# The first 512 columns of the gate's v input: seven block products in four steps among q and k, and their layer norm on VectorE

## The chip, the cores and the metric

The kernel runs on one core of a Trainium2 chip. The metric is the device time of one execution in microseconds. Before the change it is 2023.53 us, the median of three runs (2023.32 to 2023.73). TensorE (PE in the profile) multiplies; VectorE (DVE), ScalarE (ACT) and GpSimd (POOL) prepare its operands and take its results from the accumulators in PSUM; SyncE (SP) issues the loads of the weights.

## The reference, cut to what matters

A trunk of two layers on 256 positions of width 2048, all in float32. What the change touches is the first projection of each layer and the gate fed by its last columns:

```
for l in range(DEPTH):                      # 2
    h = rms_norm(x, norm1_g[l])             # (1, 256, 2048)
    z = h @ w_in[l]                         # w_in[l]: 2048 x 5120
    q, k, v, gu, gv = jnp.split(z, splits, axis=-1)     # 1024 columns each
    attn = dilated_attention(rotary(q), rotary(k), v)   # 8 heads of 128
    gm = chunked_gmlp(gelu(gu), gelu(gv), ln_g[l], ln_b[l], w_spatial[l], b_spatial[l])
    x = x + concat([attn, gm]) @ w_out[l]
    x = x + square(relu(rms_norm(x, norm2_g[l]) @ w_up[l])) @ w_down[l]

def chunked_gmlp(u, v, ln_g, ln_b, w_s, b_s):
    v = layer_norm(v in 8 groups of 128 columns, ln_g, ln_b)
    sp = (lower triangle of w_s) @ v + b_s  # in each group and each chunk of 128 positions
    return u * sp
```

The first 512 columns of gv are the first four of its eight groups.

## The kernel before, in words

**Three products for one.** Every weight tile is 128 x 1024 float32 (512 KB). SP loads it into `raw` (7 buffers); ACT rounds it to a high part `hi` (`Sub.high`, 6 buffers), VectorE subtracts and rounds to a low part `lo` (`Sub.low`, 6 buffers). PE forms hi·hi, lo·hi and hi·lo in its rounded float32. The activations have such parts as well: `hs` holds x times the norm's gain in both.

**A list of steps.** The function `layer` writes a list `steps`; the loop at the end walks it, and every engine gets its instructions in that order and executes them in that order. Each step issues, in turn: the high parts of tiles up to five ahead, whatever `soon` has made due, the low parts up to four ahead, the loads, its own matmuls, and then what hangs on it (`after`, hooks, and the queue that `later` fills). A mark is a step with no tile. An instruction that has to wait holds up all that stands behind it on its engine.

**Kinds of steps.** `transposed` has the weights stationary: one tile is 24 matmuls of 256 columns, four tiles make a group of 256 output columns. `natural` has the activations stationary: one tile is 12 matmuls of 512 columns into two accumulators, eight tiles make 512 output columns. `fast` forms a product of 2 x 2 blocks with seven block products for eight: a step loads two tiles (`Top`, `Bottom`), makes two more from their sums (`Sums`, upper and lower: four subtractions of 512 elements on VectorE, then high and low parts), and runs 42 matmuls of 256 columns; the last two are issued inside the next step. It needs activations and their block sums in high and low parts. Before the change only the second MLP product uses it, with block sums of the hidden activations that `sums` makes.

**The first stage of a layer.** v runs first (`natural`, 16 tiles), then k and q by turns (`transposed`, 4 groups each, 32 tiles; I call them places 0 to 31), then gv (`natural`, 16 tiles), then gu (`transposed`, 16 tiles), then the product with `w_out`. When a q or k group ends, `after_qk` rotates it (two ACT copies, three VectorE operations); two steps behind a q group `scores` runs, then `normalise`, `turn` and `values` for that pair of heads. When half of gv ends, `after_gv` takes it out of PSUM and through the gelu; `stats` and `layer_norm` follow, `layer_norm` on POOL; `spatial` (PE) needs the normed groups while gu runs.

**Accumulators.** PSUM has eight banks of 512: `acc0` to `acc3` for the steps, four `aux` for the small products of the attention and the norms.

Of the kernel before, what the change touches and what calls it, by code (L numbers as in the profile page):

```python
# [68 lines left out]
BEHIND, BETWEEN = 2, 1  # L69
D_SCORES, D_NORM, D_TURN, D_VALUES = 2, 1, 3, 2  # L70
# [21 lines left out]
def trunk(ctx: ExitStack, tc: tile.TileContext, layout, xT, consts, gains, w, b_sp, w_sp, out):  # L92
# [9 lines left out]
    paux = ctx.enter_context(tc.tile_pool(name="paux", bufs=4, space=bass.MemoryType.PSUM))  # L102
# [37 lines left out]

    def aux_bank():
        return paux.tile([P, 512], F32, name="aux", tag="aux")
# [223 lines left out]
    def sums_ready():  # L366
        run_until(lambda: summed[0])
# [46 lines left out]
    def fast(name, l, row0, col0, tiles, slots, fresh, last, done):  # L414
# [6 lines left out]
        for p in range(2):  # L421
# [3 lines left out]
            def mm(p=p, top=top, bottom=bottom, upper=upper, lower=lower):  # L425
                if p == 0:
                    o.extend(slots())
                half = tiles[0][0]
                sums_ready()
                extra = sum_parts[0]  # L430
# [44 lines left out]
    def mark(fn):  # L475

        steps.append((None, fn, None))

# [39 lines left out]
    def layer(l, n1, n2, n3, last):  # L518
# [27 lines left out]
        if l:  # L546
            mark(start)
        mix_a, mix_g = [None], [None]
# [38 lines left out]
        def scores(j, q, k):  # L587
# [3 lines left out]
            s1, s0 = aux_bank(), aux_bank()  # L591
# [65 lines left out]
        def after_gv(c, ps):  # L657
            z, u = t32("gz", [2, 512], tag="tmpB"), t32("gu", [2, 512], tag="tmpA")
            for tt in range(2):
                act.activation(z[:, tt, :], ps[tt], AF.Copy, scale=n1.half[:, tt:tt + 1])  # L660

            def then(u, z):
# [5 lines left out]
                later(1, 1.5, lambda: stats(c // P))  # L668

            gelu(z, u, then)  # L670

        def stats(g0):
# [8 lines left out]
            later(0, 1.0, lambda: layer_norm(g0))  # L681

        def layer_norm(g0):
            y, mv = par["y"], par["mv"]
            r = t32("lr", [2, 4])
            rsqrt(nc.gpsimd, r, mv[:, :, g0:g0 + 4, 1], 1.0, LN_EPS, [2, 4])
            for g in range(4):
                for tt in range(2):
                    yg = y[:, tt, (g0 + g) * P:(g0 + g + 1) * P]
                    nc.gpsimd.tensor_scalar(yg, yg, mv[:, tt, g0 + g, 0:1], r[:, tt, g:g + 1],  # L690
                                            op0=OP.subtract, op1=OP.mult)
# [108 lines left out]
        def sums():  # L800

            a11, a12, a21, a22 = (inner[:, 4 * k:4 * k + 4, t * P:(t + 1) * P] for t in range(2) for k in range(2))
            vec.tensor_tensor(a22, a21, a22, op=OP.add)
            vec.tensor_tensor(a21, a11, a21, op=OP.subtract)
            vec.tensor_tensor(a11, a22, a11, op=OP.subtract)
            vec.tensor_tensor(a12, a12, a11, op=OP.subtract)
# [41 lines left out]

        def halves(bank):
            return [bank[:, 0:256], bank[:, 256:512]]  # L850
# [62 lines left out]
        for e in range(9):  # L913
# [5 lines left out]
            if e:  # L919
                w = 512 * len(ORDER.get(e, USUAL))  # L920
                hidden = [hid[e - 1]]
                down = collect(transposed, "w_down", l, (e - 1) * 1024, 8, w, D - w, from_tiles(hidden, NH),
# [3 lines left out]
                for g, at in enumerate(ORDER.get(e, USUAL)):  # L926
                    banks = []
                    quick += zip(at, collect(fast, "w_down", l, (e - 1) * 1024, 512 * g, hidden,
# [16 lines left out]
    def hook(i, fn):  # L945

        hooks.setdefault(i, []).append(fn)
# [128 lines left out]
```

## Time and profile before

| | |
|---|---|
| median of three runs | 2023.53 us |
| profiled execution: its own time / its span | 2023.7 us / 2021.9 us |
| granted TensorE clock, mean of the span | 0.997 |
| busy PE / DVE / ACT / POOL | 99% / 78% / 60% / 8% of the span |
| weights loaded | 731 tiles of 512 KB, 4.7 us from issue to landing (median) |
| HBM read and written over the span | 206 GB/s |

The page is of one execution. "Busy" is the time in which an engine executes; on PE, matmuls overlap, so that a busy PE can still be slowed by what feeds it, but not stand. An answer by windows gives, for a stretch of the span, the busy time and the instruction count of each engine; a timeline gives start, length, engine, line and shape of every instruction, and in brackets the idle time ahead of it with what ended it.

### The profile page before, as it was taken

Reading aid. Unit: us, or ns where it says so; the run is one execution under the profiler, and the core shown is the slowest. Engines: PE = TensorE matmul, PEld = TensorE weight load, DVE = VectorE, ACT = ScalarE, POOL = GpSimd, SP = SyncE. Lnnn points to the kernel's source line nnn. Section 1 sums busy time; section 2 is a strip of 40 time slices with the busy share of each in tenths; the row PEclk is TensorE's granted clock in tenths of the full one; section 3 lists DMA queues with packets and bytes.
Section 4 is the critical chain, followed back from the end, with each engine's and each line's share of the span. In section 5 each row is a group of like instructions: output and inputs, shape, how many; then the busy total and the mean of one; then the engine's idle time right before and its main releaser. Section 6 shows DMA issues by size and latency. Waiting matters only on the chain.

```text
span 2021.9 us, 40716 instructions
## 1 busy us (share of the span) xinstructions
PE 2009.5 (99%) x16810; PEld 1973.4 (98%) x16810; DVE 1579.8 (78%) x1954; ACT 1221.2 (60%) x1613; POOL 156.2 (8%) x200
## 2 busy tenths in 40 slices
PE   9999999999999999999999999999999999999997
PEld 8998999999999999999989989999999999999997
DVE  7566766688888898898856667667888898888985
ACT  7565455566566666665645654556666666667653
POOL 0002300000001000100000032000000000010000
PEclk9999999999999999999999999999999999999998
DMA  9555556566678776866664555565676776777662
GB/s 330 192 167 167 187 189 202 174 229 204 222 219 239 240 225 203 249 215 215 201 215 158 168 187 188 188 199 179 217 229 208 228 236 216 239 220 241 212 215 81
DMA packets 126442, 419.26 MB, mean 207 GB/s; under 512 B 14128, under 2 KB 22064, under 8 KB 126256
## 3 DMA queue, kind: packets, MB, share of 16 engines
q1 hardware_dynamic: 110800, 389.86, 57.2%
q0 software_dynamic: 14304, 23.86, 6.5%
q8 instruction: 131, 2.15, 0.4%
q10 hardware_dynamic: 1152, 2.94, 0.4%
q14 instruction: 55, 0.45, 0.1%
HBM read 394.58 MB, written 22.02 MB: 206 GB/s over the span
## 4 chain that ended last, share of the span: by engine, by line
PE 99%; DVE 0%; ACT 0%; issue 0%; DVEq 0%
PE acc L410 70%; PE acc L440 10%; PE aux L440 8%; PE acc L470 3%; PE acc L472 3%; PE acc L471 3%; PE aux L699 0%; PE aux L635 0%; PE aux L593 0%; PE aux L622 0%; PE aux L994 0%; DVE x L1038 0%; PE aux L596 0%; PE aux L637 0%; PE acc L846 0%; PE aux L539 0%
## 5 line engine op out<-in xcount | busy, mean ns | idle before, releaser
L168 ACT ACTIVATE hi<-raw 128x1024 fp32r<-128x1024 f32 (+1 forms) x817 | 836.9, 1050 | 487.5 <-DVE raw L220 216.2
L178 DVE TENSOR_TENSOR lo<-raw,hi 128x1024 fp32r<-128x1024 f32 (+1 forms) x817 | 965.3, 1214 | 143.4 <-ACT hi L168 140.4
L410 PE MATMUL acc<-hs,hi 128*128 128x256 f32 x5632 | 985.9, 277 | 0.0
L410 PEld LDWEIGHTS acc<-hs,hi 128*128 128x128 f32 x5632 | 857.9, 188 | 0.4 <-issue 0.2
L410 PE MATMUL acc<-hs,lo 128*128 128x256 f32 x2816 | 778.0, 276 | 0.0
L410 PEld LDWEIGHTS acc<-hs,lo 128*128 128x128 f32 x2816 | 528.7, 188 | 0.4 <-issue 0.2
L410 PE MATMUL acc<-half,hi 128*128 128x256 f32 x2688 | 462.2, 276 | 0.0
L410 PEld LDWEIGHTS acc<-half,hi 128*128 128x128 f32 x2688 | 406.7, 188 | 0.0
L410 PE MATMUL acc<-half,lo 128*128 128x256 f32 x1344 | 371.0, 276 | 0.0
L410 PEld LDWEIGHTS acc<-half,lo 128*128 128x128 f32 x1344 | 252.3, 188 | 0.0
L873 POOL DMA_DIRECT2D far<-ar x92 | 74.2, 816 | 1164.4 <-ACT ar L876 563.9
L440 PE MATMUL acc<-hi,shared 128*128 128x256 f32 x768 | 138.4, 276 | 0.0
L440 PEld LDWEIGHTS acc<-hi,shared 128*128 128x128 f32 x768 | 119.2, 188 | 0.0
L440 PE MATMUL aux<-hi,half 128*128 128x256 f32 x528 | 110.6, 276 | 0.0
L440 PE MATMUL acc<-lo,shared 128*128 128x256 f32 x384 | 106.0, 276 | 0.0
L649 DVE TENSOR_TENSOR half<-ar,half 128x512 fp32r<-128x512 f32 x72 | 49.8, 691 | 68.6 <-ACT half L646 68.6
L470 PE MATMUL acc<-hi,hs 128*128 128x512 f32 x256 | 101.8, 398 | 0.0
L472 PE MATMUL acc<-hi,hs 128*128 128x512 f32 x256 | 100.6, 393 | 0.0
L471 PE MATMUL acc<-lo,hs 128*128 128x512 f32 x256 | 100.3, 392 | 0.0
L440 PEld LDWEIGHTS aux<-hi,half 128*128 128x128 f32 x528 | 87.2, 188 | 0.0
L440 PE MATMUL aux<-hi,shared 128*128 128x256 f32 x448 | 80.7, 276 | 0.0
L510 DVE TENSOR_TENSOR x<-x,acc 128x512 f32<-128x512 f32 (+1 forms) x49 | 33.1, 675 | 59.1 <-PE acc L410 57.3
(150 smaller groups left out, 1955.3 us busy)
## 6 DMA issues: line engine op xcount, KB each, us to landing
raw<-in_w SPq DMA_DIRECT2D x731, 512.0 KB, 4.7
far<-ar POOLq DMA_DIRECT2D x60, 256.0 KB, 8.3
far<-ar POOLq DMA_DIRECT2D x32, 128.0 KB, 4.3
ar<-far POOLq DMA_DIRECT2D x12, 256.0 KB, 9.7
raw<-in_w SPq DMA_DIRECT2D x10, 256.0 KB, 5.1
x<-in_xT SPq DMA_DIRECT2D x7, 256.0 KB, 5.9
out<-x SPq DMA_DIRECT2D x7, 256.0 KB, 3.1
shared<-in_b_sp ACTq DMA_DIRECT2D x2, 512.0 KB, 7.7
```

The lines of the kernel that those rows point to most:

```text
L168: act.activation(self.h[:, j * m:(j + 1) * m], self.raw[:, j * m:(j + 1) * m], AF.Copy)
L178: vec.tensor_tensor(lo[:, r], self.raw[:, r], self.h[:, r].bitcast(F32), op=OP.subtract)
L410: pe.matmul(o, lhsT=lhs, rhs=xs[:, rhs, :], start=(first and j == 0), stop=(last and j == 2), skip_group_check=True)
L440: calls.append(lambda k=k, j=j, lhs=lhs, rhs=rhs: pe.matmul(o[n], lhsT=lhs, rhs=rhs, start=(p == 0 and k == 0 and j == 0 and n in fresh), ...
L470: pe.matmul(ps, lhsT=xh, rhs=hi, start=(k0 + k == 0), stop=False)
L471: pe.matmul(ps, lhsT=xh, rhs=lo, start=False, stop=False)
L472: pe.matmul(ps, lhsT=xl, rhs=hi, start=False, stop=(k0 + k == KC - 1))
L510: vec.tensor_tensor(xj, xj, ps[j][:, 0:S] if alone else pair(ps)[:, j, :], op=OP.add)
L649: vec.tensor_tensor(t[:, c:c + 2, 1, :], src, t[:, c:c + 2, 0, :].bitcast(F32), op=OP.subtract)
L873: nc.gpsimd.dma_start(far[g][:, r], src, **({} if e == max(g, 1) else {"accum_op": OP.add}))
```

## The change

In both layers the first 512 columns of gv leave the stage behind q and k. They become four steps of the `fast` kind ahead of places 3, 6, 17 and 25 of q and k: the first two take the upper 1024 rows of `w_in`, the other two the lower 1024. For each half of the rows `seven_sums` makes x times the gain in float32 in a buffer `plain` (eight ACT operations) and its block sums (four VectorE operations), and `seven_parts` rounds them, two chunks at a time, to high and low parts. For the first half this is done from the 13th step of v on; for the second, a mark ahead of place 11 and four marks ahead of places 12 to 15. The seven block results stay in `acc2`, `acc3` and two of the four `aux` banks until `gather` adds them up, five steps behind the last; q and k alternate between `acc0` and `acc1` alone, and the smaller score block goes to the one of them that is free. The second half of gv stays `natural` in its old place; the first half's gelu starts ahead of its seventh tile, and its statistics and layer norm follow at once, the layer norm on VectorE. The layer norm of the second half stays on POOL.

The core of the diff (banks by name, and the helpers moved out of the MLP, are left out):

```
+SEVEN, AGAIN = ((3, 6), (17, 25)), 11
...
+    def strassen_sums(f, i, n):
+        a11, a12, a21, a22 = (f[:, 4 * k + i:4 * k + i + n, t * P:(t + 1) * P] for t in range(2) for k in range(2))
+        vec.tensor_tensor(a22, a21, a22, op=OP.add)
+        vec.tensor_tensor(a21, a11, a21, op=OP.subtract)
+        vec.tensor_tensor(a11, a22, a11, op=OP.subtract)
+        vec.tensor_tensor(a12, a12, a11, op=OP.subtract)
...
-            s1, s0 = aux_bank(), aux_bank()
+            s1, s0 = aux_bank(), acc_bank(1 - bank_at[0]) if aux_held else aux_bank()
...
+        def seven_slots():
+            if "o" not in seven:
+                banks = [acc_bank(2), acc_bank(3)]
+                for _ in range(2):
+                    banks.append(aux_bank())
+                    seven.setdefault("aux", []).append(aux_at[0])
+                aux_held.update(seven["aux"])
+                seven["o"] = [h for b in banks for h in halves(b)][0:7]
+            return seven["o"]
+
+        def seven_sums(rows):
...
+            f = seven["plain"][rows]
+            for k in range(NH):
+                c = NH * rows + k
+                act.activation(f[:, k, :], x[:, c, :], AF.Copy, scale=g_all[:, n1.g, c:c + 1])
+            strassen_sums(f, 0, 4)
+
+        def seven_parts(rows, k):
+            to_half(seven["sums"], k, seven["plain"][rows][:, k:k + 2, :])
+
+        def seven_done(o):
+            soon(5, lambda: gather(o))
+
+        def gather(o):
+            z = t32("gz", [2, 512], tag="tmpB")
+            p1, p2, p3, p5, p7, p6, p4 = o
+            c11, c12, c21, c22 = (z[:, tt, h * S:(h + 1) * S] for tt in range(2) for h in range(2))
+            act.activation(c12, p1, AF.Copy)
+            vec.tensor_tensor(c11, c12, p2, op=OP.add)
...
+            for tt in range(2):
+                act.activation(z[:, tt, :], z[:, tt, :], AF.Copy, scale=n1.half[:, tt:tt + 1])
+            aux_held.clear()
+            seven["z"] = z
...
         def layer_norm(g0):
             y, mv = par["y"], par["mv"]
             r = t32("lr", [2, 4])
-            rsqrt(nc.gpsimd, r, mv[:, :, g0:g0 + 4, 1], 1.0, LN_EPS, [2, 4])
+            e = nc.gpsimd if g0 else vec
+            rsqrt(e, r, mv[:, :, g0:g0 + 4, 1], 1.0, LN_EPS, [2, 4])
...
+        hook(base + 13, lambda: seven_sums(0))
+        for k in range(0, NH, 2):
+            hook(base + 14 + k // 2, lambda k=k: seven_parts(0, k))
+        plain = []
         for j in range(4):
-            transposed("w_in", l, 0, KC, AW + j * 256, 256, from_hs, lambda c, ps, j=j: after_qk("k", j, ps))
-            transposed("w_in", l, 0, KC, j * 256, 256, from_hs, lambda c, ps, j=j: after_qk("q", j, ps))
-        natural("w_in", l, 4 * AW, AW, after_gv)
+            for name, col in (("k", AW), ("q", 0)):
+                plain += collect(transposed, "w_in", l, 0, KC, col + j * 256, 256, from_hs,
+                                 lambda c, ps, j=j, name=name: after_qk(name, j, ps), of=2)
+        quick = {}
+        for rows in range(2):
+            quick.update(zip(SEVEN[rows], collect(fast, "w_in", l, 1024 * rows, 4 * AW, seven_forms(rows), seven_slots,
+                                                  () if rows else (0, 2, 4, 6), range(7) if rows else (),
+                                                  seven_done if rows else None)))
...
+        for i, one in enumerate(plain):
+            if quick.get(i):
+                steps.append(quick[i])
+            if i == AGAIN:
+                mark(lambda: seven_sums(1))
+            if AGAIN < i <= AGAIN + 4:
+                mark(lambda k=2 * (i - AGAIN - 1): seven_parts(1, k))
+            steps.append(one)
+        late = collect(natural, "w_in", l, 4 * AW + 512, 512, lambda c, ps: soon(1, lambda: after_gv(512, ps)))
+        for i, one in enumerate(late):
+            if i == 6:
+                mark(lambda: gate_half(0, seven["z"]))
+            steps.append(one)
```

Where instructions stand now, at the places that the prediction speaks of. Lines are those of each version; `lo` L178 before is L183 after.

VectorE in layer 0 behind the first pair of heads' scores (between places 9 and 13), before: the low part of a tile, the reciprocal of the softmax sums, a low part, the rotation of the second k group (three rows), a low part.

```order
L178 TENSOR_TENSOR lo_902<-raw_666,hi_854 128x1024
L611 RECIPROCAL den_891<-den_891 128x4
L178 TENSOR_TENSOR lo_937<-raw_701,hi_900 128x1024
L579 TENSOR_TENSOR ar_80<-acc3_829,cosR_553 128x512
L580 TENSOR_TENSOR ar_80<-ar_80,sinR_554 128x512
L581 TENSOR_TENSOR ar_80<-ar_80 128x512
L178 TENSOR_TENSOR lo_972<-raw_732,hi_935 128x1024
```

The same place after:

```order
L183 TENSOR_TENSOR lo_1060<-raw_912,hi_1012 128x1024
L626 RECIPROCAL den_1049<-den_1049 128x4
L485 TENSOR_TENSOR plain_502<-plain_502 128x4x128
L486 TENSOR_TENSOR plain_502<-plain_502 128x4x128
L487 TENSOR_TENSOR plain_502<-plain_502 128x4x128
L488 TENSOR_TENSOR plain_502<-plain_502 128x4x128
L183 TENSOR_TENSOR lo_1107<-raw_914,hi_1058 128x1024
L594 TENSOR_TENSOR ar_80<-acc1_987,cosR_567 128x512
L595 TENSOR_TENSOR ar_80<-ar_80,sinR_568 128x512
L596 TENSOR_TENSOR ar_80<-ar_80 128x512
L664 TENSOR_TENSOR half_503<-plain_502,half_503 128x2x256
L183 TENSOR_TENSOR lo_1144<-raw_916,hi_1105 128x1024
```

The four block sums (L485 to L488) stand between the reciprocal and the low part of place 15's tile (`lo_1107`); the first low part of the sums (L664) stands ahead of the low part of place 16's (`lo_1144`).

VectorE further on, up to the fourth tile of the step ahead of place 17, after (L224 to L229 are the four sums of `Top` and `Bottom`, `lo_1251` and `lo_1286` the low parts of the upper and the lower sum, L594 to L596 the rotation of the second q group):

```order
L664 TENSOR_TENSOR half_503<-plain_502,half_503 128x2x256
L183 TENSOR_TENSOR lo_1215<-raw_950,hi_1185 128x1024
L224 TENSOR_TENSOR raw_918<-raw_918 128x2x256
L225 TENSOR_TENSOR raw_918<-raw_950,raw_918 128x2x256
L228 TENSOR_TENSOR raw_950<-raw_950,raw_918 128x2x256
L229 TENSOR_TENSOR raw_950<-raw_950 128x2x256
L664 TENSOR_TENSOR half_503<-plain_502,half_503 128x2x256
L183 TENSOR_TENSOR lo_1251<-raw_918,hi_1219 128x1024
L594 TENSOR_TENSOR ar_80<-acc0_1148,cosR_567 128x512
L595 TENSOR_TENSOR ar_80<-ar_80,sinR_568 128x512
L596 TENSOR_TENSOR ar_80<-ar_80 128x512
L183 TENSOR_TENSOR lo_1286<-raw_950,hi_1249 128x1024
```

None of these but the rotation stood here before; there, the low parts of the next places' tiles did.

ACT at the first of these places, after: the exponentials of the first pair of heads, a high part, the two rows of `normalise`, the eight rows of `plain`, a high part, the copies of the second k group.

```order
L621 ACTIVATE ar_80,den_1049<-ar_80,mx_1048 128x256 x2
L621 ACTIVATE ar_80,den_1049<-ar_80,mx_1048 128x128 x2
L173 ACTIVATE hi_1058<-raw_914 128x1024
L629 ACTIVATE ar_80<-ar_80,den_1049 128x256 x2
L629 ACTIVATE ar_80<-ar_80,den_1049 128x128 x2
L717 ACTIVATE plain_502<-x_84,cols_82 128x256 x8
L173 ACTIVATE hi_1105<-raw_916 128x1024
L592 ACTIVATE ar_80<-acc1_987 64x512
L593 ACTIVATE ar_80<-acc1_987 64x512
```

The row with the eight operations is new here; all others stand as before in this order.

More of the change, by code (lines that the diff above doesn't have):

```diff
@@ L412, in transposed, with fast @@
             steps.append((wt, mm, (lambda c=c: after(c, accs[c])) if k0 + 4 == nk else None))
-    def fast(name, l, row0, col0, tiles, slots, fresh, last, done):
+    def fast(name, l, row0, col0, forms, slots, fresh, last, done):
         o = []
@@ new lines, in seven_forms @@
+        def seven_forms(rows):
+            return lambda: (hs[:, NH * rows:NH * (rows + 1)], seven["sums"])
+        def seven_sums(rows):
+            if "sums" not in seven:
+                f = tp.tile([P, 2, NH, S], F32, name="plain", tag="half", bufs=2)
+                seven["plain"] = [f[:, i, :, :] for i in range(2)]
+                seven["sums"] = tp.tile([P, NH, 2, S], F32R, name="half", tag="half", bufs=2)
+            f = seven["plain"][rows]
[3 more added lines that the diff above has]
+            strassen_sums(f, 0, 4)
@@ L800, in sums @@
         def sums():
[L802 to L806, printed above, removed]
+            strassen_sums(inner, 0, 4)
             def parts(k):
```

49 lines of the change are left out of this document (36 added, 13 removed).

## The prediction

> **What bounds the kernel now.** First the page's busy times and the chain that ended last, then what PE waited for, then busy times by windows.
>
> ```profile
> PE 2009.5 (99%) x16810; PEld 1973.4 (98%) x16810; DVE 1579.8 (78%) x1954; ACT 1221.2 (60%) x1613; POOL 156.2 (8%) x200
> PE 99%; DVE 0%; ACT 0%; issue 0%; DVEq 0%
> PE aux L328 <- DVE nr L354: 1.2, 1, 1.2
> 100.00:150.00 50.00, 50.00 (x426) 49.46 (x426) 32.08 (x40) 30.19 (x54) 0.00 (x0) 1.00 0.53 163
> 500.00:600.00 100.00, 100.00 (x883) 100.00 (x883) 86.60 (x97) 66.41 (x84) 7.46 (x10) 1.00 0.71 230
> 800.00:900.00 100.00, 100.00 (x883) 100.00 (x882) 90.30 (x107) 66.48 (x86) 10.59 (x12) 1.00 0.73 225
> ```
>
> The reader is to see three things. PE is the bound: the chain is PE alone, and between its start and the end of the last product it waits for nobody (the one wait shown is in the final norm). So the time changes by the PE time that goes, and by every wait that is new; nothing else can gain. Second, in the MLP VectorE works 87 to 90 us of each 100 and PE still does not wait (in a window row VectorE's busy time is the third pair, ACT's the fourth). Third, where q and k run, VectorE has 32 us of work in 50: that is the room the change fills.
>
> **What PE saves.** The removed half of gv is 8 tiles of 12 matmuls of 512 columns, 96 a layer, 192 in all. The four steps are 4 x 42 = 168 matmuls of 256 columns a layer, 336 in all. The pace of the first kind comes from an undisturbed stretch of gv:
>
> ```profile
> 157.85 0.40 PE L472 MATMUL acc<-hi,hs 128*128 128x512 f32 x1
> 168.17 0.40 PE L472 MATMUL acc<-hi,hs 128*128 128x512 f32 x1
> ```
>
> There are 45 matmuls between these two starts: 10.32 / 45 = 0.2293 us each. The second kind runs at 100 / 883 = 0.1133 us (the row 800 to 900, in which such steps stand among `transposed` ones). So 192 x 0.2293 - 336 x 0.1133 = 44.0 - 38.1 = **5.9 us saved**. The Trainium skill, page "TensorE: Matmul & The Clock Gate", section "Back-to-back issue gap", gives N / 2.4 + 2.5 ns for warm matmuls, that is 215.8 and 109.2 ns; by it the saving would be 4.7 us (an estimate from that page). The rows here are slower by 4 to 6%, for the long ones more, and I take them.
>
> **What VectorE gets.** Per layer: 16 weight sums and 8 block sums of 512 elements, 8 low parts of block sums, 7 additions of 256, low parts of the new tiles, and the layer norm of four groups; ACT gets 16 copies of 256, 8 high parts of 512 and the new tiles' high parts. In the mean that fits. Whether PE waits is decided by order, so I add up VectorE's queue at the place where most stands in one piece: places 9 to 17. Zero of the clock is 75.22, where ACT takes up the q group that ends at place 7; the trace of before has the same work up to the first softmax:
>
> ```profile
> 75.22 0.60 ACT L577 ACTIVATE ar<-acc 64x512 f32<-64x512 f32 x1 [1.71 <-PE acc L410]
> 85.65 1.48 ACT L614 ACTIVATE ar<-ar,den 128x256 f32<-128x256 f32 x4
> 87.03 1.04 ACT L168 ACTIVATE hi<-raw 128x1024 fp32r<-128x1024 f32 x1
> 84.83 0.18 DVE L611 RECIPROCAL den<-den 128x4 f32<-128x4 f32 x1
> 93.60 0.37 PE L410 MATMUL acc<-hs,hi 128*128 128x256 f32 x1
> L834 ACT ACTIVATE ar<-ar,nr 128x256 f32<-128x256 f32 x24 | 10.1, 494 | 0.0
> L894 ACT ACTIVATE ar<-aux 128x256 f32<-128x256 f32 x24 | 8.8, 367 | 0.0
> ```
>
> VectorE is through with the reciprocal at 9.8. Next in its queue now is the first block sum, which needs all eight `plain` copies. ACT begins those when `normalise` is issued (87.03, at 11.8) and takes 8 x 10.1/24 = 3.4 us: 15.2. **VectorE stands for 5.4 us**, and the low parts of places 15 and 16 stand behind it. (ACT's copies are not in the trace; their bounds are 0.37 us, the copy out of PSUM of L894, and 0.49 us, the whole length of one of L834: 3.0 to 3.9 us.) From 15.2 its rows, start to start:
>
> ```profile
> 536.09 0.69 DVE L803 TENSOR_TENSOR ar<-ar 128x512 f32<-128x512 f32 x1
> 538.88 1.22 DVE L178 TENSOR_TENSOR lo<-raw,hi 128x1024 fp32r<-128x1024 f32 x1
> 540.61 1.29 DVE L649 TENSOR_TENSOR shared<-ar,shared 128x512 fp32r<-128x512 f32 x2
> 541.82 0.69 DVE L191 TENSOR_TENSOR lo<-raw,hi 128x512 fp32r<-128x512 f32 x1
> 542.42 1.28 DVE L649 TENSOR_TENSOR shared<-ar,shared 128x512 fp32r<-128x512 f32 x2
> 543.62 1.22 DVE L178 TENSOR_TENSOR lo<-raw,hi 128x1024 fp32r<-128x1024 f32 x1
> 544.76 0.68 DVE L219 TENSOR_TENSOR raw<-raw 128x512 f32<-128x512 f32 x1
> 545.48 0.69 DVE L220 TENSOR_TENSOR raw<-raw 128x512 f32<-128x512 f32 x1
> 547.54 0.68 DVE L774 TENSOR_TENSOR ar<-ar,acc 128x512 f32<-128x512 f32 x1
> 546.26 1.06 ACT L168 ACTIVATE hi<-raw 128x1024 fp32r<-128x1024 f32 x1 [4.85 <-DVE raw L220]
> 100.63 0.69 DVE L579 TENSOR_TENSOR ar<-acc,cosR 128x512 f32<-128x512 f32 x1 [4.00 <-ACT ar L578]
> 102.57 2.35 DVE L178 TENSOR_TENSOR lo<-raw,hi 128x1024 fp32r<-128x1024 f32 x2
> ```
>
> Four block sums 2.79 (536.09 to 538.88); a low part of 1024 1.14 (543.62 to 544.76); a rotation 1.94 (100.63 to 102.57); a low part of block sums 0.60; `Top`'s low part 0.60; four weight sums 2.78 (544.76 to 547.54). In the order shown: 2.79, three low parts 3.42 (places 15, 16, `Bottom`), k's rotation 1.94, three low parts of block sums 1.81, `Top` 0.60: 25.8. The weight sums: 28.5. The fourth low part of block sums waits for ACT, which has the upper sum's high part ahead of it (ready after the second weight sum, as 546.26 after 545.48: begun 27.3, 1.0 long) and its own high part: 28.9, done 29.5. **Upper low part done at 30.7** (1.22). Then q's rotation: ACT's lower high part and two copies (1.0 and twice 0.6) end at 31.1; rotation to 33.0; **lower low part done at 34.2**.
>
> PE: the row of 93.60 is the first matmul of place 14, behind `turn`: 18.4. Three places of 24 matmuls are 8.15 us: the step ahead of place 17 begins at 26.55. Its fourth product is the first with the upper sum; its low part is wanted after 19 matmuls, at 28.7, and comes at 30.7: **2.0 us of waiting**. Two products on (1.25 us, 32.0 with a matmul that needs only the high part) it wants the lower low part of 34.2: **2.2 us more**. Together 4.2 us a layer; with the copies' bounds 3.8 to 4.8.
>
> **What is late next.** Behind the steps ahead of 17 and 25 the scores run at once, and only one tile's low part is ready beyond such a step, because the next four are issued after it. The trace has the same chain:
>
> ```profile
> 105.89 1.03 PE L593 MATMUL aux<-ar 128*128 128x256 f32 x4
> 107.11 0.37 PE L410 MATMUL acc<-hs,hi 128*128 128x256 f32 x1
> 106.72 0.69 DVE L649 TENSOR_TENSOR half<-aux,half 128x512 fp32r<-128x512 f32 x1 [1.80 <-ACT half L646]
> 107.32 0.68 DVE L602 SCALAR_TENSOR_TENSOR ar<-aux,con 128x512 f32<-128x512 f32 x1
> 109.43 1.22 DVE L178 TENSOR_TENSOR lo<-raw,hi 128x1024 fp32r<-128x1024 f32 x1
> ```
>
> From the end of `values` (105.89) VectorE needs until 109.43 + 1.22 = 110.65, 4.76 us, to have the low part of the second place; PE is there after the scores (1.22), one place (2.72), the two matmuls left over (0.23) and one more (0.11), 4.28 us. 0.5 us, twice a layer.
>
> **What I cost at nothing.** The steps ahead of 3 and 6 have their block sums made during v; layer 0 is the fuller, as its norm's factor falls in the same steps:
>
> ```profile
> 45.08 4.63 DVE L178 TENSOR_TENSOR lo<-raw,hi 128x1024 fp32r<-128x1024 f32 x4
> 52.20 0.42 DVE L567 TENSOR_TENSOR cosR<-con,aux 128x256 f32<-128x256 f32 x1 [2.49 <-ACT nR L333]
> 52.94 2.36 DVE L178 TENSOR_TENSOR lo<-raw,hi 128x1024 fp32r<-128x1024 f32 x2
> 57.97 2.16 DVE L543 SCALAR_TENSOR_TENSOR shared<-aux,cols,shared 128x128 f32<-128x128 f32 x8 [2.67 <-PE aux L539]
> L543 DVE SCALAR_TENSOR_TENSOR shared<-aux,cols,shared 128x128 f32<-128x128 f32 x16 | 4.3, 343 | 5.5 <-PE aux L539 5.5
> L570 DVE TENSOR_SCALAR nhalf<-nr 128x2 f32<-128x2 f32 x2 | 0.3, 165 | 0.0
> 64.29 0.60 ACT L577 ACTIVATE ar<-acc 64x512 f32<-64x512 f32 x1 [1.66 <-PE acc L410]
> ```
>
> From 45.1 VectorE has six low parts of 1024 (6.8), `Top` (0.6), block sums (2.8), their four low parts (2.4), weight sums (2.8), the rope's 0.74 and the eight operations of L543 (2.1): 18.3 us, with 0.4 of waiting for ACT done at 63.8. PE wants the last of it 3.5 us into a step that starts one place ahead of 64.2, at 65.0. The cover is 1.2 us; the step ahead of 6 comes out alike. The layer norm on VectorE (eight operations of 128 columns that the trace does not show there: between 0.17 us, the two columns of L570, and 0.34 us, the whole length of one of L543; I take 0.27, L543 start to start; and ten as small as L570) and the gate's other work stand among the low parts of gu's first tiles, which are four places or 10.9 us ahead; were that cover gone, it would cost some 3 us a layer. POOL loses half its layer norms, and PE did not wait for them: no gain.
>
> **The sum.** -5.9 + 2 x (4.2 + 1.0) = **+4.5 us**. The profiled execution took 2023.7 us, 1.8 more than its span and 0.2 above the median of the runs; the sum holds for either, and the forecast is 2023.5 + 4.5 = 2028.0 us. About 0.2% (4 us) is what a measurement of this kernel can tell from no change, so this lies at that bound.
>
> **Rivals.**
> 1. *VectorE is in time, and the whole saving shows.* Mechanism and place: the lateness arises in the stand ahead of the first block sum at place 11. If what follows it takes 4.2 us less than my 19.0 (or the copies come that much sooner), both waits vanish; for a gain over 0.2% both layers' waits must stay under 1.9 us together. For it: the MLP's rows at 87 to 90% with no wait. Against: there, nothing makes VectorE stand 5 us and then asks for a full tile at once. Time 2023.5 - 5.9 + 0 to 1 = 2017.6 to 2018.6.
> 2. *Half of it is hidden.* One of the two waits falls away, for example q's rotation does not wait behind the lower high part: 2 to 3 us a layer, 2021.6 to 2023.6, up to the bound of no change.
> 3. *More is late.* The cover of 1.2 us ahead of places 3 and 6, or that at gu, does not hold: 1.5 to 4 us more, 2030 to 2032.
> 4. *The clock.* The windows shown have the granted clock (the third number from the end) at 1.00, and PE never stands in them. If a wait of 4 us lowered it to half for the 42 matmuls behind, each layer would lose 42 x 0.1133 = 4.8 us more: 2037.5. The Trainium skill, the same page, section "What's actually happening", says that the clock halves after an idle window of about 3.4 us; by that my two waits of 2.0 and 2.2 us with 1.2 us of work between stay short of it. No trace here shows a gap of that size in the middle of the work.
> 5. *The seven products save nothing*, since these steps run slower beside q and k than in the MLP: 2034. Their instructions are the same as there, so hardly.
>
> **How the numbers follow.** Forecast 0.45 (2026 to 2030; 0.16 of it within 4 us of no change); rival 1 0.15; rival 2 0.22; rival 3 0.12; rivals 4 and 5 0.03 each. Faster 0.15; same 0.16 + 0.22 = 0.38; slower 0.29 + 0.12 + 0.06 = 0.47. The range leaves out the lower part of rival 1, the top of rival 3 and rivals 4 and 5: 2018.3 to 2031.5.
>
> **What the profile after would show.** Right: PE idle at the seven-product lines shortly ahead of place 17 in each layer, two waits of about 2 us put down to VectorE's low parts, VectorE idle some 5 us ahead of the first block sum with ACT's `plain` as releaser, and 192 matmuls of 512 columns fewer. Wrong: a PE with no wait there (rival 1); a wait at gu's `spatial` or ahead of places 3 and 6 (rival 3); windows with a granted clock below 1.00 near 110 us (rival 4); or a pace of the new steps above 0.1133 us without waits (rival 5).

## The result, and the profile after

The changed kernel took 2041.78 us in the median of four runs (2041.65 to 2043.85), the kernel before 2023.5 us beside it: ratio 1.0093, 95% interval 1.0075 to 1.011. It is 18.3 us slower; the forecast was 4.5 us slower, with 2031.5 as the upper end of the range.

The page after, busy times and the chain that ended last; then what PE waited for (engine, accumulator and line, releaser: total us, times, longest):

```profile
PE 2019.9 (99%) x16954; PEld 1989.2 (98%) x16954; DVE 1645.4 (81%) x2084; ACT 1251.3 (61%) x1679; POOL 129.9 (6%) x158
PE 95%; DVE 3%; ACT 2%; DMA 0%; issue 0%; ACTq 0%; DVEq 0%; SPq 0%
```

```profile
PE aux L443 <- DVE lo L183: 3.7, 2, 1.9
PE acc L443 <- DVE lo L183: 2.6, 2, 1.3
PE acc L415 <- DVE lo L183: 0.9, 4, 0.2
```

PE still is the bound, and the forecast waits are there: two a layer at the seven-product lines ahead of place 17 (3.2 us a layer for the forecast 4.2) and two a layer of 0.25 us behind the steps ahead of 17 and 25. They make 7.2 us. But PE's *busy* time has grown too, by 10.4 us, where the change takes away more matmul time than it adds. The place shows in the first gu matmul and the spread of the second norm (last row: two tiny matmuls of the norm's factor, x4 in the profile), in the timeline of PE in layer 0, before:

```profile
197.63 0.40 PE L472 MATMUL acc<-hi,hs 128*128 128x512 f32 x1
197.87 0.28 PE L410 MATMUL acc<-hs,hi 128*128 128x256 f32 x1
...
340.78 0.61 PE L328 MATMUL aux<-con,nr 128*128 128x128 f32 x4
```

and after:

```profile
198.93 0.39 PE L475 MATMUL acc<-hi,hs 128*128 128x512 f32 x1
199.16 0.59 PE L650 MATMUL aux<-ar,shared 128*128 128x256 f32 x2
199.59 0.38 PE L652 MATMUL aux<-ar,shared 128*128 128x128 f32 x2
199.81 0.60 PE L650 MATMUL aux<-ar,shared 128*128 128x256 f32 x2
200.25 0.39 PE L652 MATMUL aux<-ar,shared 128*128 128x128 f32 x2
200.39 0.36 PE L415 MATMUL acc<-hs,hi 128*128 128x256 f32 x1
...
348.65 0.61 PE L333 MATMUL aux<-con,nr 128*128 128x128 f32 x4
```

From gu to the spread: 340.78 - 197.87 = 142.91 us before, 348.65 - 200.39 = 148.26 after, **5.35 us more for matmuls that the change does not touch**. Right ahead of gu stands a burst of four small float32 matmuls (lines 650 and 652, `values` of the last two heads; each is counted twice in the profile, x2). It is due two steps behind the last `turn`, as before; but before, 16 tiles of gv stood behind q and k, and 96 matmuls of 512 columns came between this burst and gu. Now there are eight tiles, and none comes between. Windows over gu and `w_out` (the first pair behind the length is PE's busy time and instruction count, the third number from the end the granted clock), before:

```profile
200.00:300.00 100.00, 100.00 (x885) 100.00 (x885) 71.78 (x100) 49.66 (x61) 19.06 (x23) 1.00 0.57 186
```

and after:

```profile
200.00:300.00 100.00, 100.00 (x851) 99.95 (x851) 76.60 (x136) 50.18 (x63) 17.58 (x21) 1.00 0.52 171
300.00:400.00 100.00, 100.00 (x868) 100.00 (x867) 62.86 (x82) 53.37 (x70) 0.00 (x0) 1.00 0.57 185
1120.00:1130.00 10.00, 6.86 (x45) 6.36 (x44) 7.68 (x10) 5.72 (x7) 0.00 (x0) 0.87 0.31 103
1130.00:1140.00 10.00, 9.85 (x74) 9.40 (x74) 6.77 (x9) 6.26 (x13) 0.00 (x0) 0.96 0.39 123
```

PE is 100% busy at full clock both times and does 885 matmuls in 100 us before, 851 after. (From 300 to 400 it is both: up to the spread the lower count, behind it the higher.) So there are **two paces of 256-column matmuls, 0.1133 us and 0.1178 us**, and nothing in the busy share tells them apart. (In `w_out`, from 260 to 330 us, where no small matmul stands, PE has 620 matmuls before and 597 after.) The last two rows show a stretch of lower clock in layer 1, right where the two long waits are: 0.13 x 10 + 0.04 x 10 us of lost clock at half speed, that is about 3.4 us at half.

### The profile page after: what moved, and what is told of

Read it like the earlier page. It is cut to its first block, busy times and chain, and to the rows that moved or that the text cites. A ratio compares the mean times of both kernels' runs of the same rounds, so it can differ in the third digit from the quotient of the medians.

```text
span 2039.9 us, 41170 instructions
## 1 busy us (share of the span) xinstructions
PE 2019.9 (99%) x16954; PEld 1989.2 (98%) x16954; DVE 1645.4 (81%) x2084; ACT 1251.3 (61%) x1679; POOL 129.9 (6%) x158
## 4 chain that ended last, share of the span: by engine, by line
PE 95%; DVE 3%; ACT 2%; DMA 0%; issue 0%; ACTq 0%; DVEq 0%; SPq 0%
PE acc L415 67%; PE acc L443 10%; PE aux L443 9%; PE acc L475 2%; PE acc L474 2%; PE acc L473 2%; DVE lo L183 1%; ACT hi L173 0%; PE aux L650 0%; PE aux L774 0%; ACT plain L717 0%; DVE half L664 0%; DMA raw<-in_w 0%; ACT ar L621 0%; DVE ar L617 0%
## 5 line engine op out<-in xcount | busy, mean ns | idle before, releaser
L183 DVE TENSOR_TENSOR lo<-raw,hi 128x1024 fp32r<-128x1024 f32 (+1 forms) x825 | 976.4, 1216 | 127.0 <-ACT hi L173 123.9
L415 PE MATMUL acc<-half,hi 128*128 128x256 f32 x2688 | 469.0, 278 | 0.0
L443 PE MATMUL aux<-hi,half 128*128 128x256 f32 x592 | 123.4, 277 | 0.0
L664 DVE TENSOR_TENSOR half<-ar,half 128x512 fp32r<-128x512 f32 x72 | 49.7, 691 | 65.2 <-ACT half L661 65.2
L443 PEld LDWEIGHTS aux<-hi,half 128*128 128x128 f32 x592 | 97.8, 188 | 0.0
L443 PE MATMUL aux<-lo,half 128*128 128x256 f32 x296 | 82.4, 278 | 3.7 <-DVE lo L183 3.7
L443 PE MATMUL acc<-hi,half 128*128 128x256 f32 x448 | 85.6, 276 | 0.0
L473 PE MATMUL acc<-hi,hs 128*128 128x512 f32 x192 | 76.2, 397 | 0.3 <-ACT hs L292 0.3
```

The lines of the kernel that those rows point to most:

```text
L183: vec.tensor_tensor(lo[:, r], self.raw[:, r], self.h[:, r].bitcast(F32), op=OP.subtract)
L415: pe.matmul(o, lhsT=lhs, rhs=xs[:, rhs, :], start=(first and j == 0), stop=(last and j == 2), skip_group_check=True)
L443: calls.append(lambda k=k, j=j, lhs=lhs, rhs=rhs: pe.matmul(o[n], lhsT=lhs, rhs=rhs, start=(p == 0 and k == 0 and j == 0 and n in fresh), ...
L473: pe.matmul(ps, lhsT=xh, rhs=hi, start=(k0 + k == 0), stop=False)
L664: vec.tensor_tensor(t[:, c:c + 2, 1, :], src, t[:, c:c + 2, 0, :].bitcast(F32), op=OP.subtract)
```

## The experiments

Two questions: what puts gu at the slower pace (theory A: the burst of small matmuls ahead of it; B: VectorE's layer norm, the banks or the traffic beside it; C: waits), and whether the waits ahead of place 17 come from the stand at ScalarE's `plain` copies (D) or from VectorE having more to do in all (E). Ratios are to the kernel of before.

**values_sooner: the last `values` burst one step earlier.**

```diff
-D_SCORES, D_NORM, D_TURN, D_VALUES = 2, 1, 3, 2
+D_SCORES, D_NORM, D_TURN, D_VALUES = 2, 1, 3, 1
```

> The changed kernel with one number: the last values burst (four small float32 matmuls, lines 650 and 652) is due one step after the last turn instead of two, so it stands 24 matmuls of 512 columns ahead of gu, and the first gu matmul follows a 512-column matmul as it did before the change. Theory A (a burst of small float32 matmuls directly ahead of gu sets PE to the slower of two paces, 0.1178 us a 256-column matmul for 0.1133, and gu, w_out and the first column of the up projection keep it): from the first gu matmul to the spread of the second norm 142.9 us in each layer as before the change, for 148.26; about 2031.1 us, 10.7 below the changed kernel. Theory B (gu and w_out are slowed by what else is new there: VectorE's layer norm, other PSUM banks, other traffic): 148.3 us again, 2041.8. Theory C (gu waits for its low halves): waits of PE there, which this does not remove; 2041.8.

Median of seven 2031.52 us, ratio 1.0047 (1.0027 to 1.0066). Six executions lie from 2029.4 to 2032.0, as theory A has it; the seventh, the profiled one, took 2044.9, and its windows over gu (layer 1; layer 0 the same) have the slower pace:

```profile
1220.00:1320.00 100.00, 100.00 (x853) 100.00 (x852) 72.75 (x112) 47.58 (x59) 17.57 (x21) 1.00 0.57 186
```

By these times one and the same program can run gu at either pace. That speaks against B and C, which give one time; and gu can begin at the slower pace with 24 matmuls of 512 columns between the last burst and it.

**idle_before_gu: the kernel of before with an idle burst of that shape.** On constants, into a bank that nobody reads:

```diff
+        def idle():
+            ps = aux_bank()
+            for h in range(2):
+                pe.matmul(ps[:, h * S:(h + 1) * S], lhsT=ident, rhs=con[:, 512:768], start=(h == 0), stop=False, ...)
+                pe.matmul(ps[:, h * S + P:(h + 1) * S], lhsT=ident, rhs=con[:, 768:896], start=False, stop=True, ...)
+
+        mark(idle)
         transposed("w_in", l, 0, KC, 3 * AW, AW, from_hs, after_gu)
```

> The kernel of before with four float32 matmuls of the shape of a values burst, on constants and into a bank that nobody reads, directly ahead of gu in each layer; nothing else differs. Theory A: if the burst sets the slower pace, as the real one does in the changed kernel, gu to spread goes from 142.9 to about 148.3 us in each layer: 2023.5 + 2 x 1.25 (the burst) + 10.7 = about 2036.7. Theory B: the bursts alone, 2023.5 + 2.5 = 2026.0, pace 0.1133.

2036.77 us (2036.46 to 2037.12, four runs), ratio 1.0066 (1.0051 to 1.0081). The same window as above:

```profile
200.00:300.00 100.00, 100.00 (x853) 100.00 (x852) 69.77 (x99) 48.49 (x60) 19.02 (x23) 1.00 0.53 174
```

853 for 885, without any part of the change: 2.5 us of burst put some 10.8 us on the matmuls behind it. The burst directly ahead of gu is enough by itself; nothing that B or C names is in this kernel.

**idle_sooner: the same idle burst 24 matmuls of 512 columns earlier.** The same `idle`, as a mark two steps ahead of the end of gv.

```diff
-        natural("w_in", l, 4 * AW, AW, after_gv)
+        for i, one in enumerate(collect(natural, "w_in", l, 4 * AW, AW, after_gv)):
+            if i == 14:
+                mark(idle)
+            steps.append(one)
```

> The kernel of before with the idle burst of four float32 matmuls two natural steps (24 matmuls of 512 columns) ahead of gu in place of directly ahead of it, where the run with the burst at gu itself took 2036.8. If a burst acts only on the 256-column matmuls that follow it directly, the fast pace in gu: 2023.5 + 2 x 1.25 = 2026.0. If it sets a state that lasts through 512-column matmuls, the slow pace: 2036.7, or the one in some executions and the other in others.

2026.26 us (2025.64 to 2027.81, ten runs), ratio 1.0015 (1.0006 to 1.0025), and gu is back at 885 in the profiled execution. A burst that stands in the 512-column matmuls leaves gu alone here, by their times in all ten executions.

**turn_before_gu: another kind of burst directly ahead of gu, in the kernel of before.**

```diff
+        def idle():
+            for h in range(2):
+                ps = aux_bank()
+                for n in range(3):
+                    pe.transpose(ps[:, n * P:(n + 1) * P], con[:, 512 + n * P:512 + (n + 1) * P], ident)
+
+        mark(idle)
```

> The kernel of before with six idle float32 transposes of 128 columns (the shape of a turn) directly ahead of gu in each layer, where four idle float32 matmuls of the shape of values gave 2036.8. If the kind of burst decides (behind turn the traces mostly show the fast pace): 2023.5 + 2 x 0.8 for the transposes = 2025.1, 885 matmuls in 100 us of gu and w_out. If any small burst directly behind 512-column matmuls sets the slow pace: 2025.1 + 10.7 = 2035.8, 853 in 100 us.

2028.77 us (2028.1 to 2029.23, ten runs), ratio 1.0025 (1.0015 to 1.0035): neither number. Windows in q and k and in gu:

```profile
100.00:150.00 50.00, 50.00 (x415) 49.58 (x414) 32.26 (x40) 29.70 (x54) 0.00 (x0) 1.00 0.48 153
...
200.00:300.00 100.00, 100.00 (x885) 100.00 (x884) 71.62 (x99) 50.95 (x63) 20.88 (x25) 1.00 0.55 180
```

gu is fast behind the transposes, as the first number had it. But q and k are slow here, 415 matmuls from 100 to 150 us for the 426 of before, though each engine has the same instructions in the same order up to gu. In the kernel of before the pace is slow from the first `scores` to the first `turn` and fast behind it; here that `turn` did not end it, in either layer: some 430 matmuls a layer at 0.0045 us more make 3.9 us, and 2028.77 is 3.7 above the first number. So the instructions alone do not decide which pace a burst leaves.

**spread_behind_values: two more tiny matmuls between the burst and gu.**

```diff
+        def reset():
+            run_until(lambda: par["heads"] == 4)
+            n1.spread(copy=False)
+
+        mark(reset)
         transposed("w_in", l, 0, KC, 3 * AW, AW, from_hs, after_gu)
```

> The changed kernel, the last values burst where it is, and directly behind it, ahead of the first gu matmul, the two tiny float32 matmuls of a norm's spread once more (0.4 us), whose result nobody reads. In the changed kernel's trace the fast pace began again right behind such a spread. Theory A: the spread sets the fast pace, gu to the next spread 142.9 us, 2041.8 - 10.7 + 2 x 0.4 = about 2031.9. If the last burst of any kind sets the slow pace, it is 2042.6. Theory B: 2042.6.

2043.06 us (2041.28 to 2044.76), ratio 1.0094 (1.0077 to 1.0111); gu at 853. The second number came: behind this spread, which follows another burst, the slow pace goes on; behind the norm's own spread, which follows 24 matmuls of 256 columns, it ends in every profile.

**pool_norm: the first half's layer norm back on GpSimd.**

```diff
-            e = nc.gpsimd if g0 else vec
+            e = nc.gpsimd
```

> The changed kernel with the first half's layer norm back on GpSimd (as before the change), all else as changed. Theory A (the burst ahead of gu sets the slow pace): gu to spread stays 148.3 us in each layer, 2041.8 +- 1. Theory B (VectorE's layer norm beside gu slows gu): gu to spread 142.9, 2031.1.

2048.77 us (2045.36 to 2054.85), ratio 1.0128 (1.0114 to 1.0143). What PE waits for, the first row:

```profile
PE aux L774 <- POOL shared L765: 8.0, 6, 1.6
```

Neither expectation has these waits: GpSimd's layer norm now comes too late for `spatial`. With them the granted clock fell, to a mean of 0.83 from 210 to 230 us, so the time decides nothing between A and B. The start of gu does: its first 120 matmuls, ahead of these waits, begin from 202.97 to 217.06 us, 0.1184 us each (layer 1 the same), for 0.1134 in the kernel of before (197.87 to 211.37). The slow pace is there without VectorE's layer norm, against B. In the changed kernel, with the layer norm on VectorE, PE has no wait at `spatial`.

**copies_two_sooner: ScalarE's copies issued with place 9, the sums where they were.**

```diff
             f = seven["plain"][rows]
 ...
-            strassen_sums(f, 0, 4)
+            if not rows:
+                strassen_sums(f, 0, 4)
 ...
+            if i == AGAIN - 2:
+                one = (one[0], lambda mm=one[1]: (seven_sums(1), mm()), one[2])
             if i == AGAIN:
-                mark(lambda: seven_sums(1))
+                mark(lambda: strassen_sums(seven["plain"][1], 0, 4))
```

> The changed kernel with ScalarE's eight copies for the second block sums issued two places sooner (with the step at place 9 instead of ahead of place 11); VectorE's sums and all of PE's order stay. Theory D (the waits of PE at the step ahead of place 17 come from VectorE standing for those copies): VectorE's idle time of about 5 us ahead of the first sum goes, PE's waits of 1.3 and 1.9 us in each layer go (6.4 us), and with them the half clock of 3.4 us in the second layer (1.7 us). That saves up to 8.1 us less what the pace gives back: the stall in layer 0 also ended a slow stretch at 115.6 us, which now may go on to the next burst, some 60 to 300 matmuls at 0.0045 us (0.3 to 1.4 us): 2034 to 2036. Rival E (the low halves are late because VectorE simply has more to do there): waits stay, 2041 to 2042.

2030.97 us (2030.79 to 2032.0), ratio 1.0038 (1.0023 to 1.0053): 10.8 us less than the changed kernel. VectorE's first block sum follows the reciprocal at once, and the stretch of layer 1 that had the low clock has none:

```profile
94.31 0.18 DVE L626 RECIPROCAL den<-den 128x4 f32<-128x4 f32 x1
94.40 0.66 DVE L485 TENSOR_TENSOR plain<-plain 128x512 f32<-128x512 f32 x1
...
1120.00:1130.00 10.00, 9.75 (x78) 9.36 (x78) 6.30 (x9) 5.89 (x13) 0.00 (x0) 1.00 0.43 141
```

Theory D: the seven-product lines no longer wait at all; in q and k only the four waits of 0.25 us stay, and two of 0.15 us at a `turn`. It saves more than the 8.1 us expected: the slow stretches in q and k got shorter too (in layer 0 they end at the first `turn` at 100 us instead of at 115.6, in layer 1 at 1123 us instead of 1164.55), and a stop costs more than its idle time, as shown below.

**both: the two edits together.**

> The changed kernel with ScalarE's eight copies two places sooner and the last values burst one step sooner. The two savings are in different stages. If the burst two steps ahead of gu leaves PE at the fast pace in both layers (six of seven executions of the run with that edit alone were at 2029.4 to 2032.0): 2031.0 - 10.7 = about 2020.3, below the kernel of before by 3. If it leaves the slow pace, as in that run's profiled execution at 2044.9 (gu to spread at 0.1178 in both layers): 2031. If there is no such pair of values, but something in between, the pace is not a lock.

Median of eleven 2027.28 us (2021.55 to 2032.17), ratio 1.0017 (1.0008 to 1.0026). Windows of layers 0 and 1 in the profiled execution of 2027.9:

```profile
200.00:300.00 100.00, 100.00 (x885) 100.00 (x884) 75.48 (x121) 49.60 (x63) 17.58 (x21) 1.00 0.59 190
1220.00:1320.00 100.00, 100.00 (x852) 100.00 (x852) 67.73 (x83) 49.30 (x63) 15.15 (x16) 1.00 0.55 185
```

One layer fast, one slow. In layer 1 the slow pace began for the last time at the restart behind one of the 0.25 us waits, at 1153.22 us, and PE had it on both sides of the last bursts and the 512-column matmuls, up to the spread at 1346.27.

**both_scores_later: the four short waits taken away as well.** The `scores` and `values` that stood between a two-tile step and the next low part go one step later:

```diff
-                later(D_SCORES, 3.0, lambda: scores(j, q, k))
+                later(D_SCORES + (j in (1, 2)), 3.0, lambda: scores(j, q, k))
```

> The run with both edits, and the scores of the second and third heads (with the values that run with them) due one step later, so that VectorE makes the second low half behind each two-tile step ahead of places 17 and 25 instead of standing 2.8 us for those values first. Theory A in its wider form (any stop of PE, the 0.25 us waits there too, can leave the slower pace, and it lasts through the 512-column steps until something ends it): the four waits of 0.25 us go (1.0 us), the slow stretch that began behind one of them in layer 1 and held until the spread at 1346 us goes, and the executions no longer spread from 2021.5 to 2032: most at 2019 to 2022. Rival (the pace that gu finds is set by the last bursts ahead of it, not by the waits): the spread of times stays, median about 2026.

Median of twelve **2018.20 us**, ratio 0.9977 (0.9969 to 0.9985). Eleven executions lie between 2017.8 and 2018.3. The twelfth, the profiled one, took 2028.3 and has gu slow in both layers:

```profile
200.00:300.00 100.00, 100.00 (x853) 100.00 (x852) 73.21 (x115) 47.57 (x59) 17.58 (x21) 1.00 0.56 185
```

There is no stop in q and k in it, and q and k end at the fast pace (there is one stop of 0.25 us a layer at the last `values` burst, as in the other profiles with that burst moved). So the short waits were one way into the slow pace, not the only one.

**one_wide: one idle matmul of 512 columns between the burst and gu,** in the changed kernel.

```diff
+        def one_wide():
+            run_until(lambda: par["heads"] == 4)
+            pe.matmul(aux_bank(), lhsT=hs[:, 0, 0, 0:P], rhs=hs[:, 0, :, :].rearrange("p a b -> p (a b)"), ...)
+
+        mark(one_wide)
         transposed("w_in", l, 0, KC, 3 * AW, AW, from_hs, after_gu)
```

> The changed kernel with the last values burst where it is and one idle matmul of 512 columns (two parts of hs, a bank that nobody reads) between it and gu. If a 512-column matmul behind the burst is enough to let the weight loads catch up, gu to spread is 142.9 us in each layer and the time 2041.8 - 10.7 + 2 x 0.23 = 2031.6. If one is not enough, or the burst's state lasts through it, 148.3 us and 2042.3.

2037.26 us (2034.31 to 2043.01), ratio 1.007 (1.0057 to 1.0083), layer 0 fast and layer 1 slow in the profile:

```profile
200.00:300.00 100.00, 100.00 (x882) 99.91 (x881) 78.80 (x137) 51.27 (x65) 17.58 (x21) 1.00 0.56 180
1220.00:1320.00 100.00, 100.00 (x853) 100.00 (x852) 71.14 (x102) 50.08 (x63) 17.58 (x21) 1.00 0.59 195
```

One wide matmul behind the burst is no sure cure: the fast pace followed it in one layer and not in the other.

**later_and_wide: all of these.** The kernel of `both_scores_later` with `one_wide`'s mark.

> The run with both edits and the later scores, and the idle matmul of 512 columns directly ahead of gu. If one such matmul ends the slow pace, 2020 + 0.5, in all executions. If it does nothing, the time of the run without it plus 0.5.

**2018.38 us** (2018.28 to 2018.76, nine runs), ratio 0.9974 (0.9965 to 0.9984). gu is fast in both layers, and PE's one wait that is not of the program's start and end is the third row:

```profile
200.00:300.00 100.00, 100.00 (x885) 100.00 (x884) 75.35 (x119) 49.54 (x63) 17.58 (x21) 1.00 0.56 190
1220.00:1320.00 100.00, 100.00 (x885) 100.00 (x884) 68.57 (x84) 51.80 (x67) 11.25 (x9) 1.00 0.60 199
...
PE aux L650 <- ACT ar L639: 0.5, 2, 0.3
```

This beats both kernels, by 5.1 us the one of before. The stop at the last `values` burst is there, and gu is fast all the same. Nine executions without an exception beside eleven of twelve do not show that the wide matmul is what made the difference.

## Why the prediction was wrong, point by point

**The failed step.** It is the sentence "So the time changes by the PE time that goes, and by every wait that is new; nothing else can gain", with 0.1133 us for every 256-column matmul. The rows of before that showed 883 in 100 us were read as *the* pace of such matmuls; they showed one of two. The matmuls that the change leaves alone cost 2 x 5.35 = **10.7 us more** in gu, `w_out` and the first column of the up projection, because the burst now ends directly ahead of them. That is most of the 13.8 us by which the forecast missed. In the order of the changed program, `values` ahead of gu could be seen, but no rival asked what it does to the matmuls behind it. And the trace of before already had the slow pace, between the first `scores` and the first `turn` of each layer. The rest of the miss, some 3 us, lies between v and gu, where the change is: there the time grew by 2.6 us in layer 0 and 5.1 us in layer 1 (last matmul of v to first of gu: 147.10 and 144.91 us before, 149.69 and 149.99 after), 7.7 us for the forecast 4.5. From the spread to the end of the next v, and from the second spread to the final norm, nothing moved by more than 0.1 us.

**Right to a tenth: VectorE's queue.** Zero of the forecast's clock, ScalarE's copy of the q group, is at 84.65 in the trace after. Rows of ScalarE, VectorE and PE at that place:

```profile
84.65 0.60 ACT L592 ACTIVATE ar<-acc 64x512 f32<-64x512 f32 x1 [1.66 <-PE acc L415]
96.52 3.29 ACT L717 ACTIVATE plain<-x,cols 128x256 f32<-128x256 f32 x8
...
99.84 0.69 DVE L485 TENSOR_TENSOR plain<-plain 128x512 f32<-128x512 f32 x1 [5.36 <-ACT plain L717]
...
114.10 1.22 DVE L183 TENSOR_TENSOR lo<-raw,hi 128x1024 fp32r<-128x1024 f32 x1
117.60 2.35 DVE L183 TENSOR_TENSOR lo<-raw,hi 128x1024 fp32r<-128x1024 f32 x2
...
111.65 0.28 PE L443 MATMUL acc<-hi,hs 128*128 128x256 f32 x1
115.37 0.38 PE L443 MATMUL acc<-lo,half 128*128 128x256 f32 x1 [1.32 <-DVE lo L183]
118.88 0.39 PE L443 MATMUL aux<-lo,half 128*128 128x256 f32 x1 [1.87 <-DVE lo L183]
```

The stand was forecast at 5.4 us and took 5.36; the copies 3.4, and took 3.29; the upper low part at 30.7, and ended at 115.32 - 84.65 = 30.7; the lower one at 34.2, and ended at 117.60 + 1.22 - 84.65 = 34.2. `copies_two_sooner` shows that the stand is the cause.

**Mis-sized: the waits, 3.2 us a layer for 4.2.** PE came later than forecast (111.65 is 27.0, for 26.55), since it ran at the slow pace from the `scores` ahead of 91.3 us on. In the profiled run `one_wide`, where layer 0 was fast from the first `turn` on, the two waits are 1.83 and 1.82 us, near the forecast 2.0 and 2.2. The small waits were forecast at 0.5 us and show 0.25. But the forecast counted from the time at which PE would have begun the next matmul, and the profile counts idle time from the end of the matmul ahead, which overlaps its follower. Rows of PE at one of them:

```profile
125.41 0.28 PE L415 MATMUL acc<-hs,lo 128*128 128x256 f32 x1
125.52 0.39 PE L415 MATMUL acc<-hs,hi 128*128 128x256 f32 x2
126.16 0.39 PE L415 MATMUL acc<-hs,lo 128*128 128x256 f32 x1 [0.25 <-DVE lo L183]
126.38 0.40 PE L415 MATMUL acc<-hs,hi 128*128 128x256 f32 x2
```

The matmul of 126.16 was due 0.1133 us behind the second of the row above it, at 125.75: it came 0.4 us late, near the forecast. Counted so, the long waits of layer 0 are 1.5 and 2.0 us, 3.5 for 4.2. And from the start at 125.41 to that at 126.38 four matmuls take 0.97 us, where 0.45 are due: **a stop costs PE about 0.27 us beyond the idle time that the profile shows**, the same at each of the eight stops but the one where the clock fell.

**The saving of 5.9 us was sound.** `later_and_wide` gains 5.1 us in all. From the last matmul of v to the first of gu it takes 144.87 and 142.68 us, 2.23 us less than before in each layer, with 0.46 us of idle matmuls and two stops of 0.4 to 0.5 us each, from start to start, in that: 5.7 to 5.9 us without them, of which 0.2 is a shorter slow stretch in q and k.

**Rival 4, the clock, came in part.** It had 4.8 us in each layer; the low clock came in layer 1 alone. PE's rows there:

```profile
1123.80 0.39 PE L443 MATMUL acc<-lo,half 128*128 128x256 f32 x1 [1.31 <-DVE lo L183]
1127.31 0.55 PE L443 MATMUL aux<-lo,half 128*128 128x256 f32 x1 [1.83 <-DVE lo L183]
...
1128.08 0.41 PE L443 MATMUL aux<-lo,half 128*128 128x256 f32 x1
...
1128.93 0.63 PE L443 MATMUL aux<-hi,hs 128*128 128x256 f32 x2
1129.36 1.05 PE L650 MATMUL aux<-ar,shared 128*128 128x256 f32 x2
...
1130.63 0.68 PE L650 MATMUL aux<-ar,shared 128*128 128x256 f32 x2
```

The starts from 1128.08 to 1128.93 are 0.213 us apart. The nine matmuls from 1127.31 to 1129.36 took 1.0 us more than at 0.1178, and the half burst from 1129.36 to 1130.63 is 0.6 us longer than its like from 199.16 to 199.81: 1.6 us. The Trainium skill, page "TensorE: Matmul & The Clock Gate", section "What's actually happening", has the clock halve after an idle window of about 3.4 us. This trace does not agree with the rule as the prediction had read it: PE stood 1.31 and 1.83 us with 1.7 us of work between, so that no 3.4 us without work came ahead of the lower clock, which then held for about 3.4 us. Nor do the waits alone decide it. In the profiled execution of `spread_behind_values`, with the same instructions up to gu, the granted clock fell at this place in both layers; in that of `one_wide` it fell in neither, with waits as long (1.83 and 1.82 us, and 1.32 and 1.83).

**The rest.** Rival 3 (more late at 3, 6 or gu) is not in the trace: no wait there. Rival 5 (the new steps slower by their kind) is not either; they run at whichever pace PE is in. POOL "no gain" was right for the kernel of before; with half of gv moved, `pool_norm` shows that a layer norm left on GpSimd makes PE wait.

**The sum after the fact.** -5.9 saved, +10.7 pace from gu to the spread, +6.3 and +0.9 waits, +1.6 clock: 13.6 of the 18.3. Slow stretches in q and k add some: 0.0045 us for each 0.1178, so 0.9 us for the 24 us from 91.3 to 115.6 in layer 0 and 2.5 us for the 65 us from 1099.75 to 1164.55 in layer 1, less the 0.9 us that the kernel of before has there (twice 12 us). The eight stops, at about 0.27 us each beyond their idle time, add 2.1 us. That makes 18.2 us of the 18.3; the parts of 1 us and less are rough, and they are read from one execution.

## What to carry to other kernels

Where the matrix engine is 100% busy, its instruction count per stretch has to be compared as well as its waits: a change can slow matmuls it does not touch. A burst of small products moved to the head of a long stage is a change to that stage, and a short stop ahead of it can be one too. And in a queue that runs in order, an operation that waits for several copies holds up all that stands behind it; the copies should be issued earlier by the time that they take. Eight copies issued two places sooner were worth 10.8 us here.

## What the runs showed of the hardware that was not expected

Matmuls of 256 columns with a weight load each ran at one of two paces, 0.1133 and 0.1178 us (885 or 853 instructions in 100 us with the small bursts among them), at a granted clock of 1.00 and with PE 100% busy. The slow pace held for up to 148 us, through the four `spatial` bursts inside gu. In the thirteen profiles it changed only at a burst of small float32 matmuls or at the restart behind a stop, never within an unbroken stretch. The pace at which q and k end does not decide that of gu: in `both` gu began as q and k had ended in either layer, but in `both_scores_later` they ended fast and gu began slow, and in `turn_before_gu` the other way round. One program took both paces, by its times in different executions (2029.4 to 2032.0 and 2044.9), and in `both` and `one_wide` in the two layers of one execution. Two programs with the same instructions up to gu took different paces in q and k.

The Trainium skill, page "TensorE: Matmul & The Clock Gate", section "Back-to-back issue gap", says that the spacing in such a stream is set by weight loads and matmuls together, pipelined through a reorder window. Two lasting orders of loads and matmuls would look like this, but the traces do not show them: at both paces each load begins 2 to 5 ns behind the start of a matmul. What differs is that at the slow pace one load in three takes 192 ns for 187 or 188. **What sets the pace at a burst stays open.**
